# A decoder block on one core: the second blocks of 15 experts at 64 places

## The chip, the cores and the metric

The kernel runs on one core of a Trainium2 chip. The core has a matrix engine, TensorE (PE; PEld is its weight load), and VectorE (DVE), ScalarE (ACT) and GpSimd (POOL); SyncE (SP) issues most DMA transfers, which 16 DMA engines carry out. Times are device microseconds (us) of one execution; lower is better.

## The reference, cut to what matters

One decoder block over 2048 tokens of width 1024: norms, two token mixers with attention, a merge, and a layer of 32 experts in four groups. The last is what the change touches. Each token picks one group, and in it two experts; an expert is a gated product with 256 hidden columns, in blocks of up to 128 tokens:

```python
def expert_block(args):
    xb, e = args
    return (jax.nn.silu(xb @ w_gate_e[e]) * (xb @ w_up_e[e])) @ w_down_e[e]
...
y_slot = yb[dest] * w_f[order][:, None].astype(yb.dtype)
y = jnp.zeros((N, D), h.dtype).at[tok[order]].add(y_slot)
```

Everything is float32. The sum of a token's two experts is added to the block's input, and a last norm gives the output.

## The kernel before, in words

The program is one list of instructions for each engine, written by a planner, Weave. Threads (Python generators) yield the time at which they could go on, by the planner's own costs (`W.op`, `W.dma`); the thread of the lowest key that is ready goes first, and what it emits stands in that order in the engines' queues. On the chip each queue runs in order and waits by semaphores. `Ring` counts buffers in the plan.

The stages: norm and input projections (to some 420 us), attention together with gate columns (to some 1700), the merge of the two mixers with the output projection, norm and routing (to some 2130), the experts (to some 2610) and the final norm. A full-precision product of two float32 operands is mostly done in three single-pass products: `split` or `apart` (L167, L171) make a rounded part on ACT and the rest by a subtraction on DVE or POOL, and `mm3` (L185) multiplies high with high, high with low and low with high. Only some products of the attention take float32 operands as they are: `pv` (L1051) and its sums (L1070), with 64 weight columns, two products side by side, one into PSUM partitions 0 to 63 and one into 64 to 127.

The experts. `route` (L1724) writes each token's two places into lists in DRAM. `lists` (L2024) ranks the experts by their number of tokens (the first two, experts 0 and 1, start earlier and keep ranks 0 and 1), and by products with a permutation (L2074) brings the lists of all 52 blocks into SBUF: one column of token numbers and one of weights for each block, a "slot". `ORDER` (L1819) holds the experts by rank with the number of their blocks, two for ranks 0 to 19 and one for 20 to 31; `SLOTS` (L1822) the blocks in the order of work. Five threads run them:

- `load` (L1927): an expert's weights come in six chunks of 512 KB, four of gate and up, two of down, over SP's queue into a ring of four raw buffers. A chunk may go out when a raw buffer is free and the same chunk of the expert two before has been used (`used`), since the split weights have two sets of buffers. `chunk` (L1951) splits it by `apart` into `wts`; the raw buffer is given back after the subtraction.
- `fetch` (L2084): an indirect DMA on POOL's queue gathers the 128 rows of a slot (L1970). Places without a token point past the end and move nothing.
- `turn` (L2092): eight transposes on PE (L2108), and a split of the result.
- `enter` (L2119): for each of eight k, three products of 512 columns (gate and up side by side), chunk by chunk as the weights come; then silu on ACT (L2140) and a product on DVE (L2143).
- `leave` (L2150): two transposes (L2162) and a split, twelve products of 512 columns for the way down, two evictions that apply the token's weight (L2188, L2191), and an indirect DMA (L1977) that adds the rows to x2 in DRAM.

`leave` has the highest priority of the four, then `turn`, then `enter`. `rest` (L2204) first runs a loop over blocks beyond those planned (as many turns as needed, which may be none), then the final norm.

The order of work without experts 0 and 1, before:

```python
for _g in range(6):
    ORDER += [(2 + 3 * _g, 2), (20 + 2 * _g, 1), (3 + 3 * _g, 2), (21 + 2 * _g, 1), (4 + 3 * _g, 2)]
```

## Time and profile before

| | us |
|---|---|
| median of three runs | 2665.09 (2662.35 to 2671.33) |
| profiled execution | 2665.63 |
| its span in the trace | 2663.9 |

The trace holds one execution. A busy time is the sum of an engine's work in a stretch; PE's ends are modelled, so the distance between starts tells more than a duration. "PEclk" is the granted clock as a share of full speed. "DMA share" is the mean busy share of the 16 DMA engines. The chain of waits is followed back from the last instruction, at each step to what released it.

### The profile page before, as it was taken

Reading aid. Unit: us, or ns where it says so; the run is one execution under the profiler, and the core shown is the slowest. Engines: PE = TensorE matmul, PEld = TensorE weight load, DVE = VectorE, ACT = ScalarE, POOL = GpSimd, SP = SyncE. Lnnn points to the kernel's source line nnn. Section 1 sums busy time; section 2 is a strip of 40 time slices with the busy share of each in tenths; the row PEclk is TensorE's granted clock in tenths of the full one; section 3 lists DMA queues with packets and bytes.
Section 4 is the critical chain, followed back from the end, with each engine's and each line's share of the span. In section 5 each row is a group of like instructions: output and inputs, shape, how many; then the busy total and the mean of one; then the engine's idle time right before and its main releaser. Section 6 shows DMA issues by size and latency. Waiting matters only on the chain.

```text
span 2663.9 us, 38518 instructions
## 1 busy us (share of the span) xinstructions
PE 2469.3 (93%) x13504; PEld 1928.7 (72%) x13504; DVE 1470.3 (55%) x3338; ACT 1070.2 (40%) x1674; POOL 1169.7 (44%) x931
## 2 busy tenths in 40 slices
PE   6999998989899899999999998999999899999991
PEld 5898886767566566677666664899888688888871
DVE  7402114757477666637776672422465566766666
ACT  5311113545333334344333333423332466666653
POOL 1012112323145556664566677444432356666650
PEclk9999998999999999999999998999999999999995
DMA  8613648676732242245322212865643479998877
GB/s 297 215 52 99 184 123 206 177 204 188 175 80 74 60 123 63 65 113 162 107 65 67 60 48 56 271 185 183 208 147 139 150 239 296 287 280 267 271 216 265
DMA packets 274682, 430.70 MB, mean 162 GB/s; under 512 B 52493, under 2 KB 184087, under 8 KB 270901
## 3 DMA queue, kind: packets, MB, share of 16 engines
q1 hardware_dynamic: 246967, 369.43, 46.0%
q0 software_dynamic: 16000, 33.63, 5.8%
q10 hardware_dynamic: 11520, 25.17, 2.5%
q8 instruction: 107, 1.75, 0.3%
q14 instruction: 88, 0.72, 0.1%
HBM read 317.18 MB, written 131.89 MB: 169 GB/s over the span
## 4 chain that ended last, share of the span: by engine, by line
PE 80%; DVE 7%; DMA 6%; POOL 3%; issue 2%; ACT 2%; SPq 1%; ACTq 0%; POOLq 0%; DVEq 0%
PE bank L321 21%; PE bank L187 10%; PE bank L189 10%; PE bank L188 10%; PE bank L1053 7%; PE bank L1001 4%; PE bank L1041 3%; PE bank L1044 3%; POOL zs L1062 2%; PE bank L1070 2%; PE bank L2108 2%; PE bank L1043 1%; PE bank L1029 1%; DMA qa<-q 1%; DMA gb<-gate 1%
## 5 line engine op out<-in xcount | busy, mean ns | idle before, releaser
L1046 ACT ACTIVATE p<-bank 128x512 f32<-128x512 f32 x458 | 266.2, 597 | 432.0 <-PE bank L1044 404.7
L180 POOL TENSOR_TENSOR fwl<-fraw,fwh 128x1024 fp32r<-128x1024 f32 x54 | 130.0, 2408 | 527.3 <-ACT fwh L174 497.9
L1062 POOL TENSOR_TENSOR zs<-zs,p 128x512 f32<-128x512 f32 x229 | 298.2, 1302 | 29.0 <-ACT p L1046 10.0
L1080 DVE RECIPROCAL rz<-bank 128x256 f32<-128x256 f32 x126 | 219.7, 1749 | 64.7 <-PE bank L1070 64.4
L321 PE MATMUL bank<-fhh,fwh 128*128 128x512 f32 x616 | 247.5, 402 | 4.1 <-ACT fwh L174 4.1
L321 PE MATMUL bank<-fhh,fwl 128*128 128x512 f32 x616 | 247.1, 401 | 1.7 <-POOL fwl L180 1.7
L321 PE MATMUL bank<-fhl,fwh 128*128 128x512 f32 x616 | 246.4, 400 | 0.0
L1053 PE MATMUL bank<-p,v 128*64 128x256 f32 x1704 | 234.5, 416 | 3.2 <-ACT p L1046 3.0
L174 ACT CAST wh<-raw 128x1024 fp32r<-128x1024 f32 x192 | 199.6, 1052 | 34.6 <-DMA raw<-in_w_gu_e_dram 22.7
L180 DVE TENSOR_TENSOR wl<-raw,wh 128x1024 fp32r<-128x1024 f32 x123 | 178.3, 1455 | 45.1 <-ACT wh L174 42.4
L180 POOL TENSOR_TENSOR wl<-raw,wh 128x1024 fp32r<-128x1024 f32 x69 | 167.3, 2425 | 81.7 <-ACT wh L174 81.2
L1044 PE MATMUL bank<-q,ka 128*128 128x512 f32 x426 | 199.6, 468 | 0.0
L1053 PEld LDWEIGHTS bank<-p,v 128*64 128x64 f32 x1704 | 124.7, 148 | 83.2 <-issue 22.7
L187 PE MATMUL bank<-wh,oh 128*128 128x512 f32 x416 | 172.4, 415 | 0.0
L1004 DVE TENSOR_REDUCE mx<-bank 128x1 f32<-128x512 f32 x192 | 128.2, 687 | 75.2 <-PE bank L1001 74.7
L1001 PE MATMUL bank<-kb,qa 96*128 96x512 f32 (+3 forms) x448 | 155.6, 378 | 9.3 <-DMA kb<-k 8.6
L189 PE MATMUL bank<-wh,ol 128*128 128x512 f32 x416 | 164.0, 394 | 0.0
L188 PE MATMUL bank<-wl,oh 128*128 128x512 f32 x416 | 163.3, 393 | 0.0
L1062 POOL TENSOR_TENSOR zs<-p 128x512 f32<-128x512 f32 x86 | 111.2, 1294 | 90.0 <-ACT p L1046 71.9
L1084 POOL TENSOR_TENSOR rz<-rz,gb 128x256 f32<-128x256 f32 x96 | 72.7, 758 | 175.8 <-DVE rz L1080 150.7
L1041 PE MATMUL bank<-qa,kb 97*128 97x512 f32 x362 | 148.7, 411 | 0.8 <-ACT qa L1031 0.7
L321 PEld LDWEIGHTS bank<-fhh,fwh 128*128 128x128 f32 x616 | 118.3, 192 | 30.9 <-ACT fwh L174 4.9
(490 smaller groups left out, 6091.5 us busy)
## 6 DMA issues: line engine op xcount, KB each, us to landing
raw<-in_w_gu_e_dram SPq DMA_DIRECT2D x128, 512.0 KB
fraw<-in_w_cols_dram SPq DMA_DIRECT2D x77, 512.0 KB
raw<-in_w_down_e_dram SPq DMA_DIRECT2D x64, 512.0 KB
xt<-in_x_dram SPq DMA_DIRECT2D x32, 512.0 KB
sg<-fo ACTq DMA_DIRECT2D x64, 256.0 KB
q<-q SPq DMA_DIRECT2D x64, 256.0 KB
sg<-sg SPq DMA_DIRECT2D x64, 256.0 KB
gb<-gate SPq DMA_DIRECT2D x64, 192.0 KB
```

The costliest lines, as they stand in the source:

```text
L180: e.tensor_tensor(out=lo, in0=src, in1=hi.bitcast(F32), op=ALU.subtract)
L187: mm(out, lhsT=wh, rhs=xh, start=first, stop=False, **kw)
L188: mm(out, lhsT=wh, rhs=xl, start=False, stop=False, **kw)
L189: mm(out, lhsT=wl, rhs=xh, start=False, stop=last, **kw)
L321: K.T.matmul(ps, lhsT=w[:, k, :], rhs=self.H[ch][x][f][:, k % 4], start=k == 0 and j == 0, stop=k == 7 and j == 2)
L1001: T.matmul(ps[:, :w], lhsT=q1[0:rows, h, :], rhs=kb[0:rows, a:a + w], start=True, stop=True)
L1041: T.matmul(ps, lhsT=kb, rhs=q1, start=True, stop=False)
L1044: T.matmul(ps, lhsT=ka, rhs=q2, start=False, stop=True)
L1046: A.activation(p, ps, AF.Exp)
L1053: T.matmul(u[hp * 64:hp * 64 + 64, 0], lhsT=v, rhs=p[:, 2 * hp:2 * hp + 2, :], start=first, stop=last, skip_group_check=True)
L1062: e.tensor_tensor(out=out, in0=a, in1=b, op=ALU.add)
L1080: V.reciprocal(r, z)
```

## The change

The second blocks of ranks 5 to 19 (15 experts) get 64 places instead of 128. Ranks 2 to 4 keep two full blocks. Each of the 15 experts now does its 64-place block first, and is followed by one of the others: ranks 20 to 31, then 2 to 4. The 64-place blocks take their operands in float32 without a split: the raw weight chunks, a copy of the transposed rows, a copy of the transposed h. With 64 places as weight columns, two products go side by side: for gate and up the first and second 128 hidden columns of both, for the way down the first and second 512 output columns. The gate and up products are issued in one piece when all four chunks are there, the down products likewise. A raw chunk is given back only when it has been both split and used by the 64-place block; for the four gate and up chunks of these experts there is a ring of four further buffers ("xf"). The rows go back by a scatter of 128 half rows of 2 KB. The lists get further columns for 64 places on both halves of the partitions, and the slot tables are set by one memset per entry.

```diff
-TWOS, ONES = 20, 12
+HALF = 64
+FULL, TWOS = 5, 20
+_halves, _others = list(range(FULL, TWOS)), list(range(TWOS, NE)) + list(range(2, FULL))
 ORDER = [(0, 2), (1, 2)]
-for _g in range(6):
-    ORDER += [(2 + 3 * _g, 2), (20 + 2 * _g, 1), (3 + 3 * _g, 2), (21 + 2 * _g, 1), (4 + 3 * _g, 2)]
+for _h, _o in zip(_halves, _others):
+    ORDER += [(_h, 2), (_o, 2 if _o < FULL else 1)]
 SLOTS = [(0, 0, 0), (1, 1, 0), (0, 0, 1), (1, 1, 1)]
-SLOTS += [(n, r, b) for n, (r, c) in enumerate(ORDER) for b in range(c) if n > 1]
+for _n, (_r, _c) in list(enumerate(ORDER))[2:]:
+    SLOTS += [(_n, _r, _b) for _b in ((1, 0) if FULL <= _r < TWOS else range(_c))]
...
+def is_half(r, b=1):
+    return FULL <= r < TWOS and b == 1
...
-    for s, (n, r, b) in enumerate(SLOTS[:4]):
+    for s, (n, r, b) in enumerate(SLOTS):
         V.memset(sr[:, s:s + 1], float(r))
         V.memset(bl[:, s:s + 1], float(b))
...
+        self.fx = K.keep("mf", bufs=4)
+        self.fR = Ring(4)
...
-            return (rawR.f and (n < 2 or used.get((n - 2, c)) and self.order is not None)
+            return ((self.fR.f if c < 4 and is_half(ORDER[n][0]) else rawR.f)
+                    and (n < 2 or used.get((n - 2, c)) and self.order is not None)
                     and (n % 2, c // 4) in self.pools)
...
-                rawR.take()
-                raw = K.raw.tile([128, 1024], F32, name="raw3")
+                if c < 4 and is_half(r):
+                    self.fR.take()
+                    raw = self.fx.tile([128, 1024], F32, name="xf")
+                else:
+                    rawR.take()
+                    raw = K.raw.tile([128, 1024], F32, name="raw3")
...
+    def raw_used(self, n, c, t):
+
+        if (n, c) in self.half_used:
+            (self.fR if c < 4 else self.K.rawR).give(max(t, self.half_used.pop((n, c))))
+        else:
+            self.half_used[n, c] = t
...
+    def scatter_half(self, y, tk):
+
+        K = self.K
+        K.G.indirect_dma_start(out=K.sc["x2"].rearrange("s (c n) -> (s c) n", c=2),
+                               out_offset=bass.IndirectOffsetOnAxis(ap=tk, axis=0), in_=y, in_offset=None,
+                               bounds_check=2 * S - 1, oob_is_err=False, compute_op=ALU.add)
...
+        for o in range(2):
+            for c in range(2):
+                for a in range(4):
+                    T.matmul(lp2[c * HALF:(c + 1) * HALF, o], lhsT=li[:, a, 0:HALF, o], rhs=perm, start=a == 0,
+                             stop=a == 3, skip_group_check=True)
...
+            if is_half(*SLOTS[s][1:]):
+                tmR.take()
+                xt = K.pairs.tile([128, 8, 128], F32R, name=f"oh{s % 2}").bitcast(F32)[:, :, 0:HALF]
+                p8 = flat(K.bank(), 8, HALF)
+                for k in range(8):
+                    T.transpose(p8[:, k, :], xg[:, k * 128:(k + 1) * 128], K.ident[0:HALF, 0:HALF])
+                t = W.op("T", 0.6)
+                self.xgR.give(t)
+
+                def copy(s=s, xt=xt, p8=p8):
+                    K.A.copy(out=xt, in_=p8)
+                    t = W.op("A", 0.5)
+                    tmR.give(t)
+                    xts[s, 0] = xts[s, 1] = xt, t
...
-                if k % 2 and b == ORDER[n][1] - 1:
+                if k % 2 and (b == ORDER[n][1] - 1 or is_half(r)):
                     used[n, k // 2] = True
...
+    def enter_half(self, s, n):
+
+        K, W, guR, raws = self.K, self.K.W, self.guR, self.raws
+        yield lambda: NEVER if (s, 0) not in self.xts or (n, 3) not in raws or not self.xp else max(
+            self.xts[s, 0][1], raws[n, 3][1], guR.ready()) + HOP
+        guR.take()
+        gu = flat(K.bank(), 2, 128)
+        W.op("T", 0.2)
+        for k in range(8):
+            w = raws[n, k // 2][0].rearrange("p (k u f) -> p k u f", k=2, u=2)[:, k % 2]
+            for g in range(2):
+                K.T.matmul(gu[g * HALF:(g + 1) * HALF], lhsT=self.xts[s, 0][0][:, k], rhs=w[:, :, g * 128:g * 128 + 128],
+                           start=k == 0, stop=k == 7, skip_group_check=True)
+            t = W.op("T", 0.43)
+            if k % 2:
+                self.raw_used(n, k // 2, t)
...
+    def leave_half(self, s, n, h, hR, yR):
...
+        p2 = K.bank()[:, 0:128]
+        T.transpose(p2, h, K.ident)
...
+        yield lambda: NEVER if not ready or (n, 5) not in raws else max(
+            ready[0], raws[n, 5][1], self.pyR.ready()) + HOP
+        self.pyR.take()
+        ps = K.bank()
+        W.op("T", 0.2)
+        for k in range(2):
+            for c in range(2):
+                T.matmul(ps[c * HALF:(c + 1) * HALF], lhsT=hh[:, k * HALF:(k + 1) * HALF],
+                         rhs=raws[n, 4 + k][0][:, c * 512:c * 512 + 512], start=k == 0, stop=k == 1,
+                         skip_group_check=True)
+            t = W.op("T", 0.86)
+            self.raw_used(n, 4 + k, t)
+        K.A.mul(out=y, in_=ps, mul=self.rows_of[s][2])
```

In `chunk` the raw buffer of a chunk of these 15 experts is given back through `raw_used`; `lead`, the number of places planned for an expert, becomes 256 for ranks under 5, 192 for 5 to 19 and 128 for the others.

## Rows read from the trace of the kernel before

**Rows 1.** The profile page: span, busy time of the engines, the DMA queues.

```profile
span 2663.9 us, 38518 instructions
...
PE 2469.3 (93%) x13504; PEld 1928.7 (72%) x13504; DVE 1470.3 (55%) x3338; ACT 1070.2 (40%) x1674; POOL 1169.7 (44%) x931
...
q0 software_dynamic: 16000, 33.63, 5.8%
```

**Rows 2.** Busy time by stage; columns: stretch, length, engines, clock, DMA share, GB/s.

```profile
core 0: us, PE busy (x) PEld busy (x) DVE busy (x) ACT busy (x) POOL busy (x), PEclk, DMA share, GB/s
200.00:400.00 200.00, 200.00 (x875) 163.98 (x874) 34.68 (x107) 29.97 (x45) 37.01 (x54) 1.00 0.50 135
2100.00:2140.00 40.00, 27.96 (x126) 22.02 (x125) 21.18 (x71) 16.09 (x24) 18.82 (x14) 0.79 0.61 174
2150.00:2560.00 410.00, 409.78 (x2008) 338.22 (x2008) 276.10 (x331) 263.90 (x381) 261.88 (x145) 1.00 0.92 280
2180.00:2200.00 20.00, 20.00 (x103) 16.67 (x102) 12.79 (x17) 13.55 (x20) 14.10 (x8) 1.00 1.00 319
2180.00:2240.00 60.00, 60.00 (x299) 49.66 (x298) 39.77 (x49) 40.88 (x58) 40.83 (x23) 1.00 0.98 312
```

**Rows 3.** Chain of waits, expert stage, in order of time: start, length, what.

```profile
2122.51 1.39 PE bank L2074 x10
...
2161.18 0.87 PE bank L2108 x8
...
2556.46 0.87 PE bank L2108 x8
...
2611.36 2.68 DMA x<-ym,toks
```

**Rows 4.** DMA view, 2150 to 2560 us: queues, issues, median us to landing.

```profile
q1 hardware_dynamic: 23643, 86.06, 60.0%
q0 software_dynamic: 12672, 28.16, 31.1%
...
raw<-in_w_gu_e_dram SPq DMA_DIRECT2D x110, 512.0 KB
raw<-in_w_down_e_dram SPq DMA_DIRECT2D x54, 512.0 KB
...
x<-ym,toks POOLq DMA_INDIRECT x44, 7.9
```

**Rows 5.** Waits of SP, 2150 to 2560 us: in total, times, longest.

```profile
SPq L1915 <- POOL wl L180: 116.5, 38, 5.9
SPq L1917 <- POOL wl L180: 46.9, 18, 4.0
```

**Rows 6.** PE in order of time, attention stage, then expert stage.

```profile
920.62 0.39 PE L321 MATMUL bank<-fhh,fwl 128*128 128x512 f32 x1
920.84 0.39 PE L321 MATMUL bank<-fhh,fwh 128*128 128x512 f32 x1
921.16 0.65 PE L1070 MATMUL bank<-zs,ones 128*64 128x256 f32 x4
...
922.29 1.52 PE L1053 MATMUL bank<-p,v 128*64 128x256 f32 x12
923.74 0.50 PE L321 MATMUL bank<-fhl,fwh 128*128 128x512 f32 x1
...
1008.22 0.60 PE L1070 MATMUL bank<-p,ones 128*64 128x256 f32 x4
1008.65 2.33 PE L1053 MATMUL bank<-p,v 128*64 128x256 f32 x20
...
2302.02 1.04 PE L2108 MATMUL bank<-ident,xg 128*128 128x128 f32 x8
2302.81 0.48 PE L187 MATMUL bank<-wh,oh 128*128 128x512 f32 x1
```

**Rows 7.** The memsets of line 1863.

```profile
L1863 DVE MEMSET ms_sr<- x4: 59/59/59, 268.2 to 268.2; 64x1 f32 x4
```

More of the change, by code (lines that the diff above doesn't have):

```diff
@@ L1879, in __init__ @@
         self.wts, self.used = {}, {}
+        self.raws, self.half_used = {}, {}
         self.entered, self.rows_of, self.gathered = set(), {}, deque()
@@ L1968, in gather @@
         K = self.K
-        xg = self.xg.tile([128, D], F32, name="xg")
+        xg = self.xg.tile([128, D], F32, name="xg")[0:tk.shape[0]]
         K.G.indirect_dma_start(out=xg, out_offset=None, in_=K.sc["h2"][0:top],
@@ L2058, in lists @@
         lead = self.lead = cp.tile([1, NE], F32, name="lead")
-        V.tensor_scalar(lead, eo[:, 1], float(TWOS), 128.0, op0=ALU.is_lt, op1=ALU.mult)
-        V.tensor_scalar(lead, lead, 128.0, None, op0=ALU.add)
+        full = cp.tile([1, NE], F32, name="leadf")
+        V.tensor_scalar(full, eo[:, 1], float(FULL), 128.0 - HALF, op0=ALU.is_lt, op1=ALU.mult)
+        V.tensor_scalar(lead, eo[:, 1], float(TWOS), float(HALF), op0=ALU.is_lt, op1=ALU.mult)
+        V.scalar_tensor_tensor(out=lead, in0=full, scalar=128.0, in1=lead, op0=ALU.add, op1=ALU.add)
         thR.give(W.op("V", 0.4, W.op("T", 0.25)))
@@ L2070, in lists @@
         tmR.take()
-        lp = flat(K.bank(), 2, NS)
+        bank = K.bank()
+        lp, lp2 = [bank[:, i * 2 * NS:(i + 1) * 2 * NS].rearrange("p (o s) -> p o s", o=2) for i in range(2)]
         for o in range(2):
             for a in range(4):
-                T.matmul(lp[:, o], lhsT=li[:, a, :, o], rhs=perm, start=a == 0, stop=a == 3)
-        K.rawR.give(W.t["T"] + 0.5)
+                T.matmul(lp[:, o], lhsT=li[:, a, :, o], rhs=perm, start=a == 0, stop=a == 3, skip_group_check=True)
+        for o in range(2):
[3 more added lines that the diff above has]
+                             stop=a == 3, skip_group_check=True)
+        K.rawR.give(W.t["T"] + 1.5)
         k = self.rows(cp, lp[:, 0], NS, 1, "s")
@@ L2078, in lists @@
         V.tensor_copy(out=w, in_=lp[:, 1])
-        t = W.op("V", 0.8, W.op("T", 1.0))
+        k2 = cp.tile([128, NS], I32, name="row2s")
+        V.tensor_scalar(k2, lp2[:, 0], 2.0, ms["row2"], op0=ALU.mult, op1=ALU.add)
+        w2 = cp.tile([128, NS], F32, name="ws2")
+        V.tensor_copy(out=w2, in_=lp2[:, 1])
+        t = W.op("V", 1.2, W.op("T", 2.0))
         tmR.give(t)
@@ L2089, in fetch @@
             xgR.take()
-            self.gathered.append((self.gather(self.rows_of[s][0], S if s > 1 else FIRST * 256), W.op("D", 1.6, W.op("G", 1.04)) + 2.1))
+            tk = self.rows_of[s][0]
+            if is_half(*SLOTS[s][1:]):
+                tk = tk[0:HALF]
+            self.gathered.append((self.gather(tk, S if s > 1 else FIRST * 256), W.op("D", 1.6, W.op("G", 1.04)) + 2.1))
     def turn(self):
@@ L2100, in turn @@
             xR.take()
+            if is_half(*SLOTS[s][1:]):
+                tmR.take()
[10 more added lines that the diff above has]
+                    xts[s, 0] = xts[s, 1] = xt, t
+                W.later(t, copy)
+                continue
             xh, xl = [K.pairs.tile([128, 8, 128], F32R, name=f"o{w}{s % 2}") for w in "hl"]
@@ L2122, in enter @@
         for s, (n, r, b) in enumerate(SLOTS):
+            if is_half(r, b):
+                yield from self.enter_half(s, n)
+                continue
             for k in range(8):
@@ L2159, in leave @@
             hR.take()
+            if is_half(r, b):
+                yield from self.leave_half(s, n, h, hR, yR)
+                continue
             p2 = flat(K.bank(), 2, 128)
@@ L2194, in leave, with copy, put @@
             hR.give(t)
-            if b == ORDER[n][1] - 1:
+            if b == ORDER[n][1] - 1 or is_half(r):
                 used[n, 4] = used[n, 5] = True
-            def put(y=y, s=s):
-                self.scatter(y, self.rows_of[s][0], S if s > 1 else FIRST * 256)
-                yR.give(W.op("D", 1.0, W.op("G", 1.04)) + 2.1)
-            W.later(t, put)
+            W.later(t, lambda y=y, s=s: self.put(y, s, yR))
+    def leave_half(self, s, n, h, hR, yR):
+        K, W, T, raws, xp = self.K, self.K.W, self.K.T, self.raws, self.xp
+        p2 = K.bank()[:, 0:128]
+        T.transpose(p2, h, K.ident)
+        hh = xp.tile([128, 2, 128], F32R, name="hmh").bitcast(F32)[:, 0]
+        ready = []
+        def copy():
+            K.A.copy(out=hh, in_=p2)
+            ready.append(W.op("A", 0.25))
+            self.thR.give(ready[0])
+        W.later(W.op("T", 0.11), copy)
+        if not yR.f:
+            yield lambda: 0.0 if yR.f else NEVER
+        yR.take()
+        y = xp.tile([128, D], F32, name="ym")[:, 0:512]
+        yield lambda: NEVER if not ready or (n, 5) not in raws else max(
[11 more added lines that the diff above has]
+        K.A.mul(out=y, in_=ps, mul=self.rows_of[s][2])
+        t = W.op("A", 0.48, t)
+        self.pyR.give(t)
+        hR.give(t)
+        W.later(t, lambda: self.put(y, s, yR))
+    def put(self, y, s, yR):
+        W = self.K.W
+        if is_half(*SLOTS[s][1:]):
+            self.scatter_half(y, self.rows_of[s][3])
+        else:
+            self.scatter(y, self.rows_of[s][0], S if s > 1 else FIRST * 256)
+        yR.give(W.op("D", 1.0, W.op("G", 1.04)) + 2.1)
     def rest(self):
```

21 lines of the change are left out of this document (14 added, 7 removed).

## The prediction

> **What bounds the kernel now.** Start with the page's busy line [rows 1]: PE 93%, every other engine at 55% or less. That is an average over unlike stages, so the next view is the stage table [rows 2]. All that the change touches runs after 2100 us, in the expert stage, but for a table set near 268 us. From 2150 to 2560 us PE is busy 409.78 of 410 us at a granted clock of 1.00. The chain of waits says the same: the eight transposes that open a block return from 2161.18 to 2556.46 us in 42 equal steps [rows 3], 395.28 / 42 = 9.41 us for one block of 128 places. So PE sets the pace and the saving looks plain. But the last columns of [rows 2] are the warning: the DMA engines are 0.92 busy over these 410 us, and 0.98 over the 60 us from 2180 to 2240. The stage has a second limit just under the first.
>
> What that limit is made of is in the DMA view [rows 4]. The hardware queue (weights) took 60.0% of 410 us = 246 us for 110 + 54 = 164 chunks: 1.50 us of all 16 engines per chunk. The software queue (gathers and scatters) took 31.1% = 127.5 us for 28.16 MB: 4.53 us per MB. The waits of SP [rows 5] show what paces the loads: 116.5 us and 46.9 us of waiting ended with POOL's subtraction, the instruction that frees a raw buffer. Four raw buffers and 164 chunks in 410 us make 2.50 us per chunk and 10.0 us for one turn of a buffer.
>
> **The change part by part.** Routing the reference's inputs gives the tokens per expert, in the kernel's ranks: 209, 200, 195 for ranks 2 to 4, 178 down to 117 for 5 to 19, 111 down to 82 for 20 to 31. Second blocks of ranks 5 to 19 therefore hold 50 rows at most, 162 in all. They fit into 64 places, and the loop for overflow still takes no turn.
>
> *Half block on PE.* A full block has 36 matmuls and 10 transposes in its 9.41 us [rows 3]. A half has 8 + 2 pairs of full-precision products on two column halves, with 256 and 512 moving columns. The trace has this very form in the attention stage, 128x64 weights and 256 columns on each half [rows 6]: from 1008.22 to 1008.65 us one pair takes 0.43 us, and the 12 records (three pairs) from 922.29 to 923.74 us take 1.45, which is 3 x 0.43 + 0.16. The first pair after a full product starts 0.32 us after it (920.84 to 921.16) where 0.22 is usual (920.62 to 920.84). With 0.10 of that and the 0.16, a piece costs its pairs plus some 0.25 us. Gate and up: 8 x 0.43 + 0.25 = 3.69. Down, with twice the columns: 2 x 0.86 + 0.25 = 1.97. The eight transposes of 64 rows move 64 columns; eight of 128 columns take 0.79 us (2302.02 to 2302.81), so the bounds are 0.40 if the moving columns set the time and 0.79 if the weights do, which stay 128 wide. I take 0.79, the value of the row. One transpose of h: 0.11. Sum 6.56 against 9.41: 2.85 us saved, times 15 = 42.8 us if PE stays the bound.
>
> The 0.25 us per piece is this trace's price for going between whole-array and half-column products. [...]
>
> *The loads.* Nothing of the weights goes: the half reads the raw chunk, the full block of the same expert still needs cast and subtraction. The gathers and scatters move only valid rows (the 33.63 MB of the whole run are 4096 rows of 4 KB, twice [rows 1]), so a 64-place block moves the same bytes; its scatter has 128 half rows, as many entries on POOL's queue as now. The new order makes 15 pairs: half block, full block, block of another expert; the last three pairs end on ranks 2 to 4 and have one full block more. A pair in this order costs DMA 12 x 1.50 = 18.0 us for weights, and over the first twelve pairs 2855 tokens / 12 = 238 rows, each gathered and scattered at 4 KB: 1.95 MB x 4.53 = 8.8 us. That is 26.8 us. PE would need 2 x 9.41 + 6.56 = 25.4 us, where it now takes 3 x 9.41 = 28.2. So **the bound passes from PE to DMA** in these twelve pairs. Bounds of a pair: 25.4 us (PE), and above 28.2 us if the loads cannot be kept going. I take DMA at the fullest share that the stage shows for 60 us, 0.98 [rows 2]: 26.8 / 0.98 = 27.35 us, nearest to the DMA rows because these are the same loads. Saved: 12 x 0.88 = 10.6 us. In the last three pairs PE needs 3 x 9.41 + 6.56 = 34.8 us against DMA's 30.1 (326 rows): PE bound, 3 x 2.85 = 8.6 us.
>
> *The added wait.* A half waits for all four of its gate and up chunks before its first product. PE runs in order, so behind it stand the full block of the same expert, whose products mark weight buffers as used, and through those marks SP's loads two experts on; ACT and DVE wait for PE's banks. This is why a late chunk costs PE whole gaps, not overlap.
>
> *Other engines.* A half drops four of its six subtractions and casts on tiles of PSUM and one of two evictions; DVE and ACT are at 276 and 264 of 410 us [rows 2], so this pays nothing by itself.
>
> *Ahead and behind.* The lists get 16 more products, 32 records; ten of the present ones took 1.39 us on the chain [rows 3], so 0 (if the first gathers wait for the old products alone) to 4.4 us; 2.2 taken, the pairs filling both halves. PE is busy 27.96 of the 40 us around it [rows 2], so the chain has no cover there. The last block now has 67 rows to scatter where it had none: 67 x 4 KB x 4.53 = 1.2 us, with the row's 2.68 us on the chain [rows 3] as what stays; 0 to 5.2 us (a scatter's median landing of 7.9 us [rows 4] less 2.68), 1.5 taken. Some 90 more memsets of 59 ns on DVE near 268 us [rows 7] are hidden by DVE's idleness, 34.68 us busy of 200 [rows 2]; without it they would cost 5 us. The four new buffers are in space that is free by then.
>
> Sum: -10.6 - 8.6 + 2.2 + 1.5 = -15.5 us. The profiled execution took 2665.63 us (span 2663.9 and 1.7 around it), 0.5 over the median. 2665.6 - 15.5 = **2650 us**.
>
> **The rivals.**
> *PE stays the bound (2626 us).* If the eight buffers keep the DMA engines fuller and their per-chunk time falls, or the start's reserve lasts, all 42.8 us come: 2665.6 - 42.8 + 3.7. For it: 319 GB/s in the 20 us with a share of 1.00, against a mean of 280 [rows 2]. At 319 a pair's 8.24 MB would take 25.8 us. Against it: even so the pair stays above PE's 25.4, and over the 60 us from there on it was 312 GB/s, 26.4 us a pair.
>
> *The loads fall behind (2676 us, slower).* The place is SP's queue at the raw buffers. The half reads its down chunks raw, so two of the four old buffers are held from arrival until the half's down products: gate and up 3.7, silu, product, transpose and copy 1.3, down 2.0, some 7 us longer than now. Six turns of 10.0 and two of 17.0 over four buffers make 23.5 us, and the next half's four chunks stand behind them in the same queue: with nothing overlapped 4 x 1.50 = 6.0 more, 29.5 us a pair. Twelve pairs lose 15, the last three win 8.6, and 3.7 are added: +10. It decides from 28.65 us a pair. What SP now waits for [rows 5] speaks for it; against it, in the new order PE waits just where these buffers are held, so the half runs the moment its chunks are there. [...]
>
> *The halves don't run side by side (2703 us).* Then a pair costs 0.86 and 1.71 us, a half 11.7 us, 15 x 2.3 + 3.7 = +38. The rows of the attention stage have the same shape, so this has little chance.
>
> **How the numbers follow.** About 0.3%, 8 us, is what a measurement of this kernel can tell from no change. Forecast 0.45, with its own range 2642 to 2661 (0.36 of it faster, 0.09 same); PE bound 0.17; loads behind 0.33 (2660 to 2690: 0.14 same, 0.19 slower); no overlap 0.05. Faster 0.53, same 0.23, slower 0.24. The range goes to 2626 below and to 2680 above; half of the PE case, the upper end of the loads case and the last rival are left out.
>
> **What would show it.** Right: half blocks with pairs 0.43 us apart; a DMA share of 0.97 or more where 0.92 stood; PE with gaps of 2 us a pair, ended by a raw chunk from DMA; a pair every 27.4 us. Wrong on the gain side: PE without gaps and 25.4 us a pair. Wrong on the loss side: a DMA share under 0.92 with PE idle ahead of each half and a granted clock under 1.00. Wrong altogether: pairs of 0.86 us, or a time outside 2626 to 2680.

## The result, and the profile of the changed kernel

The changed kernel took **2686.45 us** (median of 4 runs, 2681.87 to 2691.71) against 2665.52 for the kernel before: ratio **1.0077**, 95% interval 1.0051 to 1.0102. A second comparison with the experiments below gave 1.0089 (1.0062 to 1.0115). So it is slower by some 21 to 24 us. The forecast was 2650; the time lies 6 us above the upper end of its range.

The page of the changed kernel, profiled in its quickest run (2681.87 us):

```profile
span 2680.1 us, 38696 instructions
...
PE 2452.8 (92%) x13581; PEld 1865.2 (70%) x13581; DVE 1425.9 (53%) x3354; ACT 1064.9 (40%) x1676; POOL 1173.5 (44%) x923
```

PE is less busy than in [rows 1] by 16.5 us, and the span is 16.2 us longer: PE has won work and lost more in waiting. The stage table says where; its columns are those of [rows 2], and the last line is one piece of half-block products, for its clock:

```profile
core 0: us, PE busy (x) PEld busy (x) DVE busy (x) ACT busy (x) POOL busy (x), PEclk, DMA share, GB/s
...
2150.00:2560.00 410.00, 375.20 (x1961) 267.72 (x1960) 222.27 (x250) 249.97 (x367) 254.74 (x138) 0.96 0.81 267
...
2386.00:2391.40 5.40, 5.40 (x34) 3.11 (x34) 0.42 (x1) 0.37 (x1) 2.07 (x1) 0.68 1.05 315
```

From 2150 to 2560 us PE works 375.20 of 410 us where it worked 409.78 [rows 2]. The DMA share fell as well, from 0.92 to 0.81. Neither of the two limits that the prediction weighed is reached. The price of a half block can be read from PE in order of time (start, length, line, form, count, and in brackets the idle time before and what ended it); the first line is the last of the gate columns (L321, the end of the attention stage), the last line the last of the experts' products:

```profile
1668.86 0.39 PE L321 MATMUL bank<-fhh,fwl 128*128 128x512 f32 x1
...
2357.63 3.67 PE L2219 MATMUL bank<-xf,oh 128*64 128x256 f32 x32
...
2364.85 0.27 PE L2298 MATMUL bank<-ident,hm 128*128 128x128 f32 x1
...
2368.02 1.94 PE L2319 MATMUL bank<-raw,hmh 128*64 128x512 f32 x8
...
2382.99 0.72 PE L2157 MATMUL bank<-ident,xg 64*128 64x64 f32 x8
2385.63 0.44 PE L2256 MATMUL bank<-ident,hm 128*128 128x128 f32 x2 [1.92 <-DVE hm L2234]
2386.00 5.36 PE L2219 MATMUL bank<-xf,oh 128*64 128x256 f32 x32
...
2621.42 0.40 PE L189 MATMUL bank<-wh,hml 128*128 128x512 f32 x1
```

Gate and up (L2219; 32 records are eight pairs of products), one transpose of h, down (L2319), the eight transposes of 64 rows (L2157): 3.67, 0.27, 1.94 and 0.72 us. But 7 of the 15 gate and up pieces took 5.36 us, like that at 2386.00; its clock was 0.68 in the stage table, after PE had stood 1.92 us ahead of L2256; the piece at 2357.63 had 1.00. The length of the stand alone does not decide it: behind 1.70 us one piece took 5.36 us and another 3.67, and behind 2.27 us one took 3.67. The first pieces of pairs 1 and 13 start at 2150.30 and 2504.49 us: 354.19 / 12 = **29.5 us a pair**, where three full blocks took 28.2 [rows 3].

What PE waited for, from 2160 to 2480 us (in total, times, longest):

```profile
PE bank L2256 <- DVE hm L2234: 22.4, 11, 3.0
```

PE stands at the transposes of h (L2256) of the full block ahead of a half, until VectorE has made that h; its gaps of about 2 us do not end with a raw chunk itself. But they hang on the chunks: ahead of the piece at 2386.00 VectorE first split two of the half's own chunks that had just landed (2382.66 to 2385.24), and in pairs 3 to 12 the piece starts 0.1 to 0.8 us after the last of its four chunks has landed, by the landings in the trace.

The DMA view of 2150 to 2560 us (queue: packets, MB, share of 16 engines; then issues and their count):

```profile
q1 hardware_dynamic: 22691, 82.66, 53.2%
...
raw<-in_w_gu_e_dram SPq DMA_DIRECT2D x54, 512.0 KB
raw<-in_w_down_e_dram SPq DMA_DIRECT2D x52, 512.0 KB
xf<-in_w_gu_e_dram SPq DMA_DIRECT2D x52, 512.0 KB
```

158 chunks took 53.2% of 410 us, 1.38 us each, against 1.50 in [rows 4]. The queues have room, at a DMA share of 0.81. What held the loads is in SP's waits over the same stretch (in total, times, longest), beside [rows 5]:

```profile
SPq L1924 <- DMA raw<-in_w_gu_e_dram: 108.1, 12, 11.0
SPq L1924 <- DVE wl L180: 96.4, 36, 14.9
...
SPq L1924 <- POOL wl L180: 26.9, 4, 21.7
```

Where the longest wait was 5.9 us, there are now waits of 11 to 22. One pair of SP's queue in order of time shows their place:

```profile
2349.23 2.77 SPq L1926 DMA_DIRECT2D raw<-in_w_down_e_dram  x2
2352.75 16.72 SPq L1924 DMA_DIRECT2D raw<-in_w_gu_e_dram  x4
2371.77 0.92 SPq L1926 DMA_DIRECT2D raw<-in_w_down_e_dram  x2
```

The two down chunks of a half's expert go out at 2349.23 and keep two of the four raw buffers. The next four chunks, gate and up of the other expert, take SP 16.72 us, since two buffers serve them. SP's waits from 2352 to 2375 us:

```profile
SPq L1924 <- DMA raw<-in_w_gu_e_dram: 10.3, 1, 10.3
SPq L1924 <- DVE wl L180: 4.9, 3, 3.8
SPq L1926 <- POOL wl L180: 3.9, 2, 2.1
```

The third of the four chunks goes into the buffer of the first: it waits 10.3 us until that has landed and 3.8 us until VectorE has split it. The fourth takes the buffer of the half's first down chunk, whose products begin at 2368.02. The load behind them goes at 2371.77, after a subtraction on GpSimd. Then the loads go out close together, and the cycle begins again. PE's gap repeats here 11 times, 22.4 us in total, and ahead of it SP stands at the raw buffers: so far the trace speaks for too few buffers; the experiments say how far.

Last, GpSimd's queue at the first gather behind the lists and at the end of the stage:

```profile
2122.66 1.06 POOL L1996 DMA_INDIRECT xg<-h,toks  x1 [8.25 <-DVE ws L2120]
...
2606.43 1.55 POOL L2009 DMA_INDIRECT x<-ym,row2s  x1 [6.06 <-DMA x<-ym,toks]
2609.98 1.56 POOL L2003 DMA_INDIRECT x<-ym,toks  x1 [1.99 <-DVE eb L2368]
2617.04 1.55 POOL L2003 DMA_INDIRECT x<-ym,toks  x1 [5.51 <-DVE ym L2282]
2624.19 1.55 POOL L2003 DMA_INDIRECT x<-ym,toks  x1 [5.60 <-DMA x<-ym,toks]
```

The last four scatters follow each other by 3.6 to 7.2 us; the last waits 5.60 us for the one before to land. In [rows 3] the last had no rows to move and took 2.68.

Two profiles of either kernel (one of each from the chip of the experiments) put the loss in three stretches. From the last product of the gate columns to the first gather behind the lists: 446.8 and 444.7 us before, 453.4 and 450.9 after, so **+6.4**. From there to PE's last product: 485.4 and 484.4 against 499.1 and 499.3, **+14.3**. From there to the end of the span: 54.1 and 54.6 against 58.3 and 57.8, **+3.7**.

### The profile page after: what moved, and what is told of

The parts are those of the page before. It is cut to its first block, busy times and chain, and to the rows that moved or that the text cites. A ratio compares the mean times of both kernels' runs of the same rounds, so it can differ in the third digit from the quotient of the medians.

```text
span 2680.1 us, 38696 instructions
## 1 busy us (share of the span) xinstructions
PE 2452.8 (92%) x13581; PEld 1865.2 (70%) x13581; DVE 1425.9 (53%) x3354; ACT 1064.9 (40%) x1676; POOL 1173.5 (44%) x923
## 4 chain that ended last, share of the span: by engine, by line
PE 72%; DMA 9%; DVE 7%; issue 4%; POOL 4%; ACT 2%; SPq 1%; ACTq 0%; POOLq 0%; DVEq 0%
PE bank L321 21%; PE bank L187 8%; PE bank L188 8%; PE bank L189 8%; PE bank L1053 7%; PE bank L1001 4%; PE bank L1041 4%; PE bank L1044 3%; POOL zs L1062 2%; PE bank L1070 2%; PE bank L2219 2%; PE bank L1043 1%; DMA x<-ym,toks 1%; POOL wl L180 1%; DMA qa<-q 1%
## 5 line engine op out<-in xcount | busy, mean ns | idle before, releaser
L180 POOL TENSOR_TENSOR fwl<-fraw,fwh 128x1024 fp32r<-128x1024 f32 x54 | 130.2, 2412 | 528.0 <-ACT fwh L174 519.3
L321 PE MATMUL bank<-fhh,fwh 128*128 128x512 f32 x616 | 246.1, 400 | 5.0 <-ACT fwh L174 5.0
L321 PE MATMUL bank<-fhh,fwl 128*128 128x512 f32 x616 | 246.5, 400 | 1.7 <-POOL fwl L180 1.7
L321 PE MATMUL bank<-fhl,fwh 128*128 128x512 f32 x616 | 246.1, 399 | 0.0
L180 DVE TENSOR_TENSOR wl<-raw,wh 128x1024 fp32r<-128x1024 f32 x90 | 129.3, 1468 | 33.1 <-ACT wh L174 31.4
L174 ACT CAST wh<-raw 128x1024 fp32r<-128x1024 f32 x132 | 137.1, 1053 | 12.3 <-DMA raw<-in_w_down_e_dram 8.2
L321 PEld LDWEIGHTS bank<-fhh,fwh 128*128 128x128 f32 x616 | 117.6, 191 | 32.1 <-ACT fwh L174 5.7
L321 PEld LDWEIGHTS bank<-fhh,fwl 128*128 128x128 f32 x616 | 117.5, 191 | 27.5 <-issue 3.5
L321 PEld LDWEIGHTS bank<-fhl,fwh 128*128 128x128 f32 x616 | 117.4, 191 | 24.9 <-issue 3.1
L188 PE MATMUL bank<-wl,oh 128*128 128x512 f32 x296 | 119.0, 402 | 11.0 <-POOL wl L180 6.0
L321 PE MATMUL bank<-hl,fwh 128*128 128x512 f32 x312 | 125.0, 401 | 1.6 <-DVE hl L180 1.6
```

The source lines that it names most:

```text
L180: e.tensor_tensor(out=lo, in0=src, in1=hi.bitcast(F32), op=ALU.subtract)
L188: mm(out, lhsT=wh, rhs=xl, start=False, stop=False, **kw)
L321: K.T.matmul(ps, lhsT=w[:, k, :], rhs=self.H[ch][x][f][:, k % 4], start=k == 0 and j == 0, stop=k == 7 and j == 2)
```

## Experiments

All are edits of the changed kernel unless told otherwise; ratios are to the kernel before, on the same chip. "Pair" is taken as above, between the first gate and up pieces of pairs 1 and 13 (order_end: pairs 4 to 15); without half blocks it is a twelfth of the time for the same 36 blocks. The two stretches are those just named, from one profile each.

| run | ratio (95%) | pair, us | gather to PE's last | to the end |
|---|---|---|---|---|
| before_same | 1.0009 (0.9997 to 1.0021) | 28.3 | 484.4 | 54.6 |
| after_same | 1.0089 (1.0062 to 1.0115) | 29.5 | 499.3 | 57.8 |
| late | 1.0166 (1.0142 to 1.0191) | 30.3 | 520.7 | 57.8 |
| planned_later | 1.0142 (1.0125 to 1.0159) | 30.5 | 508.1 | 58.5 |
| order_end | 1.0104 (1.0082 to 1.0125) | 30.0 | 509.0 | 57.0 |
| no_half | 1.0053 (1.0037 to 1.0070) | 28.7 | 486.5 | 57.3 |
| lists_only | 1.0035 (1.0022 to 1.0049) | 28.6 | 487.3 | 54.4 |
| six | 1.0051 (1.0031 to 1.0070) | 28.9 | 487.7 | 59.6 |
| broken | 1.0064 (1.0044 to 1.0085) | 28.8 | 492.5 | 57.8 |
| six_broken | 1.0028 (1.0015 to 1.0042) | 27.5 | 473.4 | 57.9 |
| no_pool | 1.0099 (1.0073 to 1.0125) | 29.3 | 492.2 | 60.3 |
| before_no_pool | 0.9991 (0.9977 to 1.0005) | 28.5 | 485.1 | 55.2 |
| six_no_pool | 0.9976 (0.9960 to 0.9992) | 27.5 | 465.2 | 59.1 |
| six_no_scatter | 0.9944 (0.9925 to 0.9963) | 26.6 | 456.3 | 58.9 |
| scatter_later | 1.0030 (1.0014 to 1.0047) | 28.2 | 484.5 | 57.4 |
| six_later | 1.0090 (1.0072 to 1.0109) | 29.4 | 495.6 | 58.9 |
| best | 0.9910 (0.9891 to 0.9929) | 26.4 | 459.4 | 57.7 |
| best_later | 0.9951 (0.9934 to 0.9967) | 26.8 | 460.1 | 57.6 |

### The two kernels again

before_same is the kernel before, after_same the changed one, both unaltered.

> The kernel before itself, with a profile from the same chip as the runs beside it: 1.000 of the kernel before, within 0.3%. It gives the spans of the stages against which the other profiles of this chip are read.

> The changed kernel itself on the chip of the other experiments: 1.005 to 1.010 of the kernel before (1.0077 was measured elsewhere). From the lists' first product to PE's last about 503 us and from there to the end about 58 us (the 64.6 us in an expectation above took an earlier product for the last one), against 487 and 54 in the kernel before.

Both came as expected. They are the scale for the rest.

### Is it ScalarE's order? (theory Q)

In the trace of the changed kernel a silu of ScalarE often stands behind casts that wait for their loads, and VectorE's product h waits for it. Two edits move silu and casts against each other, in opposite directions. The first, **late**:

```
-        self.act(s, gu, t)
+        W.later(t, lambda: self.act(s, gu, t))
...
-        K.A.mul(out=y, in_=ps, mul=self.rows_of[s][2])
...
+        def evict():
+            K.A.mul(out=y, in_=ps, mul=self.rows_of[s][2])
...
+        W.later(t0, evict)
```

> The half block's products stay in two unbroken pieces, but ScalarE's silu and its scaled eviction are issued only when the order by due times comes to them, so that casts of chunks that land during a piece stand ahead of them in ScalarE's queue. Theory Q (queue order: the silu, issued together with the piece, holds ScalarE and with it the casts for 4 to 5 us a half block; buffers come free late, loads stop, the next block's silu and PE wait): the pair falls from 29.7 to about 28 us, 15 pairs by 1.0 to 1.7 us, so 2662 to 2672 us, and ScalarE's idle time ahead of L2231 behind PE shrinks. Theory B (buffers: the half block keeps raw buffers of its down chunks and SP waits for those): no change, 2683 to 2690 us. Theory O (the order of the experts and the end of the stage): no change either.

It got worse by about 0.8%. From 2160 to 2530 us (columns as in the stage table), PE lost clock and time:

```profile
2160.00:2530.00 370.00, 334.56 (x1750) 235.38 (x1749) 228.71 (x238) 218.85 (x320) 222.54 (x118) 0.95 0.82 267
```

The changed kernel had 341 us and a clock of 0.96 there (after_same). The second, **planned_later**, raises the price of a load in the order by due times, so that casts are written later:

```
-                self.chunk(n, c, raw, W.dma(0.52))
+                self.chunk(n, c, raw, W.dma(0.62 if n > 1 else 0.52))
```

> Only the price of an expert's chunk in the order by due times is raised by a fifth (0.52 to 0.62 of its unit, from the third expert on), so that the casts of landed chunks are written later into ScalarE's queue, behind the silus and evictions that now stand behind them. Theory Q2 (since the loads set the pace, each cast waits for its landing and holds the silu behind it on ScalarE; the later silu leaves PE idle ahead of L2256 and cold at L2219): the pair falls from 29.5 to 28 to 29 us, 8 to 18 us less, 2660 to 2672 us on this chip. Theory B (what is scarce is buffers, and the loads wait for them): no gain, within 5 us of the changed kernel, or worse, as buffers come free later still.

Worse too, by 0.5%. The price also sets when the half's own pieces are due (`raws[n, 3][1]`), so this run moves more than the casts. Neither version of theory Q finds support: a later silu costs, and later casts, with later pieces, cost as well. It fits that a cast is a step of a buffer's return. The queues of ScalarE and VectorE are where PE's wait is seen; where the shortage comes from, the runs below have to tell.

### Is it the order of the experts, the end, the lists? (theory O)

**order_end** puts the two-block experts first and the smallest last, **no_half** keeps the order and the lists but halves nothing, and **lists_only** takes the order of the kernel before as well:

```
-_halves, _others = list(range(FULL, TWOS)), list(range(TWOS, NE)) + list(range(2, FULL))
+_halves, _others = list(range(FULL, TWOS)), list(range(2, FULL)) + list(range(TWOS, NE))
```

```
...
 def is_half(r, b=1):
-    return FULL <= r < TWOS and b == 1
+    return False
...
-        V.tensor_scalar(full, eo[:, 1], float(FULL), 128.0 - HALF, op0=ALU.is_lt, op1=ALU.mult)
+        V.tensor_scalar(full, eo[:, 1], float(TWOS), 128.0 - HALF, op0=ALU.is_lt, op1=ALU.mult)
```

> Only the order of the experts beside the halves changes: ranks 2 to 4 (two full blocks) come first and the smallest expert last, as before the change. Theory O (the last scatters, each waiting for the one before to land, follow one another with full blocks of rows, 64.6 us from PE's last product to the span's end against 54.0 before): the end falls back to 54 to 57 us, the stage ahead of it is the same, 2676 to 2680 us. Theories Q and B: the pairs keep their 29.7 us; without a gain at the end 2684 to 2689 us.

> The new order of experts and the lists with their extra products stay, but no block is halved: every second block has 128 places in split operands, through the shared raw buffers, as before. If the half blocks' own handling costs the time (theories Q and B): before plus lists and end, 2667 to 2678 us, under the changed kernel. If the order by itself costs it (theory O and more): 2684 us or over. The pairs should be about 28.2 us again, PE-bound.

> The order of experts is that of the kernel before and no block is halved; the lists keep their 32 extra products, the second row numbers and weights and the 104 memsets. If these are priced as forecast: 2 to 5 us over the kernel before, ratio 1.001 to 1.002. If the 1.0053 of the kernel without halves comes from them and not from the order: 1.004 or over.

The end did not move (57.0 us): the 64.6 in the expectation was a misreading, the end had grown by 3.7 us alone. It is 57.0 to 58.3 us where the last block has rows to scatter (the changed kernel, order_end, no_half) and 54.1 to 55.2 where it has none (before, before_no_pool, lists_only). Two-block experts first made the pairs no better (30.0 us), so theory O falls for the stage. Without halves, PE is the bound again in the new order, from 2160 to 2530 us:

```profile
2160.00:2530.00 370.00, 366.78 (x1782) 299.01 (x1781) 246.89 (x288) 248.20 (x354) 252.40 (x135) 1.00 0.91 285
```

the pair is 28.7 us, 0.5 over what was expected, and the stretch from the gathers to PE's last product is 486.5 us, 2.1 over before_same. The halves alone turn 486.5 into 499.3: **the loss in the stage is theirs**. But lists_only is 1.0035 without any half or new order, 6 to 13 us where the forecast had 2.2. Its four scatters of the lists leave GpSimd over 6.3 us, where before_same took 3.9 (start, length, line; idle before and its end in brackets):

```profile
2105.70 2.03 POOL L1806 DMA_INDIRECT list<-iw,si  x1 [0.78 <-DVE run L1800]
2108.04 0.96 POOL L1806 DMA_INDIRECT list<-iw,si  x1 [0.30 <-DMA raw<-in_w_down_e_dram]
...
2112.01 1.34 POOL L1806 DMA_INDIRECT list<-iw,si  x1 [0.30 <-issue]
```

Of the 6.4 us ahead of the first gather in the changed kernel, 2.4 are these scatters (6.7 us from routing's last step, L1800, to the fourth, against 4.3, in both pairs of profiles). From the fourth to the first gather it is 10.9 us on the mean before and after, although the extra products take 2.3 of them: the wait for the list's load ends sooner behind its stretched scatters (7.4 us from the fourth, against 8.5, in the first pair of profiles). With a bank of their own the first gather comes right behind the old products, but after 7.8 us in best and 11.3 in best_later (both below), so the load before them varies by more than the bank saves. The other 4.1 us are there by routing's last step (432.1 and 428.9 us after the last product of the gate columns, against 435.2 and 433.9); what they come from **stays open**. The 104 memsets held up VectorE's next instruction by 1.1 us (273.33, due at 272.25 by its steps of 5.60) and shifted PE by 1.3 us near 300 us; behind the attention stage, whose last gate column ends at 1669.3 us where it ended at 1677.6 before, nothing of that can be seen.

### Do the loads wait for buffers? (theory B)

**six** gives the half's expert six buffers of its own, for its down chunks too, so that the four raw buffers are all for the others:

```
-        self.fx = K.keep("mf", bufs=4)
-        self.fR = Ring(4)
+        self.fx = K.keep("mf", bufs=6)
+        self.fR = Ring(6)
...
-                if c < 4 and is_half(r):
+                if is_half(r):
...
-            (self.fR if c < 4 else self.K.rawR).give(max(t, self.half_used.pop((n, c))))
+            self.fR.give(max(t, self.half_used.pop((n, c))))
...
```

> All six chunks of an expert with a half block go to a ring of six buffers of their own, so none of the four shared raw buffers is held until a half block's down products. Theory B (the shared buffers held by the half's down chunks stop the loads): SP's gaps of about 16 us a pair close, the pair falls to about 28 us, 2662 to 2672 us. Theory Q (the casts stand behind the silu on ScalarE, so the other expert's buffers are late whatever the half's are): under half of that, 2678 to 2688 us.

The ratio lies between the two theories, 1.0051; but the stage gave back 11.6 of its 14.9 us (487.7). So the hold on the shared buffers was most of the stage's loss, and a second hold remains: a pair still takes 28.9 us. (The edit also raises the buffers from eight to ten; a run with ten shared ones, which would tell the number from the sharing, was not made.) SP's longest waits, from 2160 to 2530 us, now end with GpSimd's subtraction:

```profile
SPq L1926 <- POOL wl L180: 112.1, 12, 22.4
```

SP issues four chunks of the other expert, and the fifth goes 20 us later:

```profile
2322.82 4.10 SPq L1924 DMA_DIRECT2D raw<-in_w_gu_e_dram  x4
2346.82 0.92 SPq L1926 DMA_DIRECT2D raw<-in_w_down_e_dram  x2
```

while GpSimd, from 2334.4 on, stands 5.63 us at a scatter (L2003) until the one before has landed, then issues a gather and only at 2344.42 runs the subtractions (L180) that free the raw buffers:

```profile
2340.04 2.29 POOL L2003 DMA_INDIRECT x<-ym,toks  x1 [5.63 <-ACT oh L174]
2342.63 1.76 POOL L1996 DMA_INDIRECT xg<-h,toks  x1 [0.30 <-ACT hmh L2303]
2344.42 4.74 POOL L180 TENSOR_TENSOR wl<-raw,wh 128x1024 fp32r<-128x1024 f32 x2
```

**broken** issues the half's gate and up products in four pieces, one a chunk, each as its chunk lands; **six_broken** does both:

```
+        for k in range(8):
+            if k % 2 == 0:
+                yield lambda: NEVER if (s, 0) not in self.xts or (n, k // 2) not in raws or not self.xp else max(
+                    self.xts[s, 0][1], raws[n, k // 2][1], 0.0 if k else guR.ready()) + HOP
...
```

> The gate and up products of a half block are issued in four pieces of one chunk each, every piece as soon as its chunk is due to land, instead of one unbroken piece behind the last of four. Theory B (the loads wait for buffers that the half block returns late and all at once): the first buffers come back earlier, the pair falls below 29.5 us, 5 to 12 us off the changed kernel. Theory U (the unbroken piece is right: PE pays at each change between products in full precision and in split operands): 45 more changes on PE at up to 0.5 us, 0 to 20 us over the changed kernel.

> Six buffers for the expert with a half block and its products in four pieces. Theory B: what is left of SP's standstills in the kernel with six buffers (up to 22 us at one load, for a chunk of the expert's own ring) shrinks with the earlier return, 4 to 10 us below the kernel with six buffers (1.005), about 1.002. Theory U: as much slower as in the run with four buffers.

Theory B held in both, theory U in neither: the pair fell to 28.8 and 27.5 us. Sixty pieces in place of fifteen cost less than they bring. What they bring need not be the buffers' return alone: the first pieces also fill PE's wait for h, which is gone in broken, so these two runs do not tell the two apart.

### GpSimd's queue (theories P)

Both with six buffers: **six_no_pool** sends the subtraction of every weight chunk from the third expert on to VectorE; **six_no_scatter** leaves out the half blocks' scatters, so that its output is not complete:

```
-        K.W.later(t, lambda: K.apart(hi, lo, raw, t, 1024, done, pool_ok=True))
+        K.W.later(t, lambda: K.apart(hi, lo, raw, t, 1024, done, pool_ok=n < 2))
```

```
         if is_half(*SLOTS[s][1:]):
-            self.scatter_half(y, self.rows_of[s][3])
+            yR.give(W.t["T"])
+            return
```

> Six buffers, and from the third expert on the second half of each chunk's split (wl) always on VectorE (1.45 us) and never on GpSimd (2.4 us, behind scatters that wait). Theory B in its sharper form (a buffer's return is held up on GpSimd's queue: SP waits 112 us in 370 for POOL wl): 4 to 10 us below the kernel with six buffers. Against it: VectorE, busy 0.65 of these stretches, gets about 0.2 more and h's product on it comes later: 5 to 15 us above.

> Six buffers; the half blocks' weighted rows are not added to the output (15 scatters left out, their outputs are missing). Theory P (GpSimd stands at each half scatter until the one before has landed and holds its wl behind it, and the scatters' bytes take the queues' time): the pair falls to 28 us or less, 8 to 15 us below the kernel with six buffers. Theory B (buffers and the loop of loads alone): 0 to 4 us, of which most at the end of the stage.

Both gained more than expected: 20 and 28 us below six, to 0.9976 and 0.9944. With the scatters out, GpSimd keeps its subtractions and PE still runs 361.87 of 370 us:

```profile
2160.00:2530.00 370.00, 361.87 (x1955) 262.97 (x1954) 269.88 (x285) 239.76 (x350) 218.04 (x113) 1.00 0.92 306
```

Here 306 GB/s at a share of 0.92 stand against 280 at 0.92 in [rows 2].

Is GpSimd's queue enough by itself, and did the change bring it? **no_pool** is that edit on the changed kernel with its four shared buffers, **before_no_pool** on the kernel before.

> The changed kernel as it is, with its four shared buffers, and only the wl of the chunks from the third expert on always on VectorE. Theory P1 (GpSimd's queue alone is the cause: its wl stand behind scatters and hold the buffers): as large a gain as with six buffers, 15 to 25 us off the changed kernel, 0.998 to 1.003 of the kernel before. Theory P2 (it takes both, since with two of four buffers held until the half's down products the loads stand still anyway): under 8 us, 1.005 or over.

> The kernel before with its wl from the third expert on always on VectorE. If GpSimd's queue is a trouble that the change brought (theory P1 or P2): no gain, 0.999 to 1.003, since PE is the bound there and VectorE has room. If it held the kernel before as well: 0.990 to 0.997, and the 20 us that the same edit gave the kernel with six buffers say nothing of the change.

No gain in either ratio (no_pool's stage is 7 us shorter in its profile, 492.2 against 499.3). So GpSimd's queue is not a burden that the kernel before had, and for this edit **it takes both** (P2): it was worth 20 us with six buffers and nothing while two of four are held. In no_pool GpSimd just stands at the scatters instead, from 2160 to 2530 us:

```profile
POOL x L2003 <- ACT ym L2285: 142.8, 19, 11.6
```

**scatter_later** leaves everything as changed, but writes the half's scatter 5 us later into GpSimd's queue; **six_later** does it with six buffers:

```
-        W.later(t, lambda: self.put(y, s, yR))
+        W.later(t + 5.0, lambda: self.put(y, s, yR))
```

> The changed kernel; only the half blocks' scatters are written 5 us later into GpSimd's queue by due time, so that gathers and wl stand ahead of them and the scatter before has landed when GpSimd comes to them. Theory P1: less standing on GpSimd and earlier buffers, 5 to 15 us off the changed kernel. Theory P2 or B: within 4 us of it.

> Six buffers, wl still on GpSimd, and the half blocks' scatters 5 us later in its queue. If what the 15 half scatters cost there is GpSimd standing behind the scatter before (without them the kernel with six buffers fell from 1.005 to 0.994): most of it comes back, 0.995 to 0.999. If it is their bytes on the queues: little, 1.002 to 1.005.

scatter_later gained 14 to 16 us, as P1 said and P2 did not (within 4 us). So neither theory holds in both runs, and what GpSimd's queue costs with four buffers **stays open**. One thing that neither edit moves by itself is the gathers, which stand in the same queue as the scatters. With the subtractions earlier, SP's wait is now put down to the half's down products (L2319) themselves, the first hold laid bare:

```profile
SPq L1924 <- PE bank L2319: 127.8, 12, 14.5
SPq L1924 <- POOL wl L180: 46.5, 13, 21.8
```

six_later went the wrong way, 1.0090 where 0.995 to 1.005 was expected. GpSimd no longer waits at the half's scatter (L2009), but 5.3 to 5.5 us at the full block's behind it (L2003):

```profile
2323.91 1.61 POOL L2009 DMA_INDIRECT x<-ym,row2s  x1 [0.31 <-issue]
...
2333.47 1.58 POOL L2003 DMA_INDIRECT x<-ym,toks  x1 [5.53 <-DVE wl L180]
...
2353.23 1.60 POOL L2009 DMA_INDIRECT x<-ym,row2s  x1 [0.31 <-issue]
...
2362.55 1.57 POOL L2003 DMA_INDIRECT x<-ym,toks  x1 [5.30 <-DVE wl L180]
```

The standing was moved, not removed. So whether the 28 us of six_no_scatter are the standing or the scatters' bytes **stays open**; six_no_pool, with every byte still moved, had 20 of them.

### What beats both

**best**: six buffers, four pieces, subtractions on VectorE, and the lists' extra products in a bank of their own:

```
+        bank2 = K.bank()
+        lp, lp2 = [t[:, 0:2 * NS].rearrange("p (o s) -> p o s", o=2) for t in (bank, bank2)]
```

> Six buffers, the half block's products in four pieces, wl on VectorE alone from the third expert on, and the lists' extra products in a bank of their own, so that the gathers wait for the first 16 products alone. If the gains add up: 8 us by the pieces and 2 us by the bank below the kernel with six buffers and no wl on GpSimd, 0.993 to 0.996. If the pieces only cured what GpSimd's queue had delayed: 0.996 to 0.998.

> The version at 0.991 with the half scatters 5 us later as well. PE is busy throughout in that version, so nothing is left for it to gain in the stage: 0.990 to 0.992. If it comes below 0.988, GpSimd still held PE somewhere.

best is at 0.9910, below both kernels and somewhat better than the sum expected. From 2160 to 2530 us PE stands still for 0.24 us, at a granted clock of 1.00:

```profile
2160.00:2530.00 370.00, 369.76 (x1988) 260.38 (x1987) 267.11 (x316) 248.72 (x367) 123.05 (x85) 1.00 0.90 296
```

This is the case that the prediction called "PE stays the bound": 26.4 us a pair, 25 us off the stretch from the gathers to PE's last product. It is 1.0 over the 25.4 of that case; the pieces are part of it (1.08, 1.95 and 1.08 us in the pair at 2348.16, for 3.67 in one). best_later, 0.9951, missed its expectation by 0.3%. Its profile shows the same stage (460.1 against 459.4 us), but best was profiled in its slowest run (2648.45 us, where the quickest took 2633.64), so the profiles can't show the difference, and what it lost is not explained; that nothing was left to gain on GpSimd agrees with it.

## Why the prediction was wrong

**The half block's price: right.** Forecast 3.69 + 1.97 + 0.79 + 0.11 us, found 3.67, 1.94, 0.72 and 0.27, the 0.27 a lone instruction that lies beside other work. The column halves run side by side: eight pairs in 3.67 us. What the forecast left out is the clock: 7 of 15 pieces took 5.36, 7 x 1.69 = 12 us. All 7 came behind waits of PE, of 1.70 to 2.96 us. In six no such piece is left, but its clock from 2160 to 2530 us is 0.97 all the same: there products behind other waits took 0.63 us in place of 0.40.

**"So the bound passes from PE to DMA": this step failed, twice.** The forecast took 26.8 us of DMA a pair at a share of 0.98, 27.35. First, the loads of the changed kernel never came near that: the share was 0.81, and SP stood up to 22 us at a buffer. Second, the floor itself was too high. In best, pairs 4 to 13 follow each other by 26.4 us, and PE hardly stops (columns as in the stage table):

```profile
2242.75:2480.74 237.99, 237.75 (x1269) 165.85 (x1269) 175.55 (x208) 160.15 (x235) 76.77 (x54) 1.00 0.94 310
```

At 310 GB/s that is the forecast's 8.2 MB a pair, and 26.4 x 0.94 = 24.8 us of full share in place of 26.8. The 1.50 us a chunk of [rows 4] were not a price: from 2160 to 2530 us a chunk took 1.37 to 1.43 us in every run with half blocks and 1.45 to 1.50 in every run without. It is not that the queue was less full: best has 1.39 at the share of 0.94, above the 0.92 of the kernel before. What lowers it stays open. Nor does the share tell the bytes: the runs moved 280, 296 and 306 GB/s at shares of 0.92, 0.90 and 0.92 (before, best, six_no_scatter).

**The rival "the loads fall behind" was what came,** with its place (SP's queue at the raw buffers), its price (29.5 us a pair, found 29.5) and its sign of a granted clock under 1.00 (found 0.96). The forecast gave it 0.33 and DMA's floor 0.45, on the argument that the half runs the moment its chunks are there. That it did, within 0.8 us in pairs 3 to 12; but the chunks came late, since SP issues them behind its stand at the raw buffers (16.72 us in the pair shown). So the argument was no argument against this rival: it told when the half runs, and not what brings the buffers back.

That the price came out to the tenth is luck. Its working has turns of 10.0 and 17.0 us and 6.0 us of loads that overlap nothing; SP's rows show 108.1 us in 12 waits for a landing, 9 us a pair, which it does not have. Nor does it have the subtractions that stand behind scatters on GpSimd, the hold that six lays bare. "As many entries on POOL's queue as now" was true and beside the point, since in the kernel before the scatters came 9.41 us apart and landed after 7.9 [rows 3, 4], while the half's comes 6.8 us behind its neighbour (2366.07 to 2372.91 in the changed kernel) and waits for that to land.

**Why the time was 10 us above even that rival's 2676.** The last three pairs were to win 8.6 us and won 2.7. From the first product of the 13th piece to PE's last product they took 117.3 us (2504.49 to 2621.82), where the same twelve blocks took 120.0 in the kernel before (2489.80 to 2609.84), whose first and last product are

```profile
2489.80 0.39 PE L187 MATMUL bank<-wh,oh 128*128 128x512 f32 x1
...
2609.38 0.46 PE L189 MATMUL bank<-wh,hml 128*128 128x512 f32 x1
```

One wait of PE there, 5.5 us, ended with a subtraction on GpSimd. The lists' part was 6.4 us (forecast 2.2, bounds 0 to 4.4), outside its bounds: the extra products take the 2.3 us that they were priced at, but the slower scatters of the lists and the 4.1 us of open origin were not in it. The end was 3.7 (1.5, bounds 0 to 5.2), the memsets nothing that remains. From the first gather to the first piece it was 1.5 us longer than before, which the forecast did not have. With the twelve pairs' 15.4 this makes 15.4 - 2.7 + 6.4 + 3.7 + 1.5 = 24.3 us, all of the difference between the profiles.

**Chances.** Slower had 0.24. The rival that ended there had the right mechanism, and its range of 2660 to 2690 held the time; the forecast's own range was cut at 2680.

## What to carry to other kernels

When a change empties the bound engine, ask what returns the buffers of the next stage's loads, step by step and queue by queue, before a transfer's busy share is taken as the new floor: SP's queue stood up to 22 us at one late buffer here. A share of the DMA engines was no price per byte (280 and 306 GB/s, both at 0.92); compare bytes per second at like shares. And try a ring of its own, large enough for all that is held, for a buffer that is read raw by a late consumer: it gave back 11.6 of the stage's 14.9 us here.

## What the runs showed that was not expected

Moving work off a queue can be worth nothing, or 20 us, by what else is short: the same line (all subtractions on VectorE) changed the time by 0.999 on the kernel before, by 1.001 on the changed one (1.0099 against 1.0089), and by 0.9925 with six buffers (0.9976 against 1.0051). Delaying one kind of scatter by 5 us gained 0.6% with four buffers and lost 0.4% with six.

A piece of eight pairs on column halves took 3.67 us at a granted clock of 1.00 and 5.36 at 0.68, both behind stands of PE of about 2 us; in the kernel before the clock was 1.00 in each stretch from 2150 us on that was read [rows 2]. And a chunk of 512 KB cost the DMA engines 1.37 to 1.43 us beside half blocks and 1.45 to 1.50 without them.
